# Decay rows of the first layer stored by head, with the mask and the first exponential held in written order

## The chip, the cores and the metric

The kernel runs on one core of one Trainium2 chip. The metric is device time in microseconds (us) of that core, from launch to end, as the median of the runs. Five engines work beside each other: TensorE (PE in the profile; PEld is its loading of weights), VectorE (DVE), ScalarE (ACT), GpSimd (POOL) and SyncE (SP), which issues most transfers. Each engine takes its own instructions strictly in order. An instruction that waits for another engine or for a transfer holds up everything behind it on its engine.

## The reference

A decoder of two layers over 1024 tokens with 1024 channels, in float32. The first layer is a gated delta rule with 8 heads; the second is windowed attention and has no part in this case. Cut to what matters here:

```python
q, k, v = split(silu(causal_conv(rms_norm(x) @ w_in)))     # per head: 128, 128 and 256 channels
beta = sigmoid(b);  g = -exp(A_log) * softplus(a + dt_bias) # log-decay by token and head
g = cumsum(g within a chunk)
decay = exp(where(tri, g[..., :, None] - g[..., None, :], -inf))
lower = where(strict, beta[..., :, None] * (k k^T) * decay, 0)
sol   = triangular_solve(I + lower, [v * beta, k * beta * exp(g)])
qk    = (q k^T) * decay
for each chunk:                                            # state S of a head
    v_new = u - w S
    o     = (q * exp(g)) S + qk v_new
    S     = S * exp(g_last) + (k * exp(g_last - g))^T v_new
x = x + (rms_norm(o) * silu(z)) @ w_out
```

So each head needs, for each of the kernel's 8 chunks of 128 tokens, a 128x128 table of exponentials of differences of summed decays. That table is what the change is about.

## The kernel before

TensorE does every product of the projections as three products of split operands (`whi`, `wlo` against `hh`, `hl`; lines 161 to 165). Its instructions run in the order in which the program writes them. On the other engines the framework's scheduler orders the work ahead of time, by priorities and by its own idea of when operands are ready, and it may put an instruction before one that was written earlier.

The first layer goes head by head. While the recurrence of head h (`head_delta`, line 613) runs, pieces of the projection of head h+1 (`head_in`, line 577) are put between its products (`interleave`, line 86), so that TensorE has something to do while the other engines prepare the next step. The recurrence has three stretches:

- the inverse of the chunk's triangle by doubling,
- the merge of two 64-blocks into one of 128 (lines 711 to 724), whose last step on ACT is the copy into `xt` at line 724,
- the scan over 8 chunks (lines 746 to 784). In each turn PE computes `sc` (line 759), ACT makes the rounded new values from it (`Z`, line 761), PE multiplies those into the state (lines 770 to 773), DVE adds them to the state `S` (line 776), ACT rounds it (`X`, line 781), and PE uses both in the next turn (lines 750 and 609 to 611).

The table of decays of a head, `dm`, is made in `decays` (line 568): SP loads the head's summed decays from DRAM (`gd`) to all 128 partitions, the same 4 KB for each (line 571), POOL masks the upper triangle (line 572), and ACT takes eight exponentials, one for each chunk (line 575). There are two buffers `dm`. The one for head h+2 is free when the merge of head h has split its own table (line 603, `dml<-dm`), and the scheduler puts load, mask and exponentials of head h+2 right there, in the scan of head h, long before they are used. So the first two loads run together at 95 us, and the other six come one in each scan of the first six heads.

ACT holds one table of functions at a time. A switch between the exponential and the silu of the convolution (lines 506, 529, 542) is an instruction of its own, ACT_TABLE_LOAD.

In `gd` the rows lie by chunk and head, row n*8+h, 512 bytes each. A head's load therefore reads, for each partition, eight pieces of 512 bytes, 4 KB apart.

Of the kernel before, what the change touches and what calls it, by code (L numbers as in the profile page):

```python
# [18 lines left out]
P = 128  # L19
T = 1024  # L20
# [6 lines left out]
# what the tensor engine is given to do, in us, while the other engines prepare a piece of the recurrence  # L27
# [29 lines left out]
def bucket_rows():  # L57
    """one-hot of the bucket of the distance (127 - u) mod 128, [32, 256]"""
    n = (127 - np.arange(256)) % P
    large = 16 + (np.log(np.maximum(n, 1) / 16) / np.log(128 / 16) * 16).astype(np.int64)  # L60
    bucket = np.where(n < 16, n, np.minimum(large, 31))
    return np.ascontiguousarray((np.arange(32)[:, None] == bucket[None, :]).astype(np.float32))


class Kernel:
# [5 lines left out]
    # work for the tensor engine is traced in the order it runs there: generators yield after every piece, and  # L71
    # pieces whose operands are still being made are put off by a number of ticks
# [13 lines left out]
    def interleave(self, front, back, share, ahead=100):  # L86
        """after each piece of front, as much of back as it asks for (times share); then what is left of back.
        What front puts on the other engines goes before what was traced shortly before it"""
        credit = 0.0
        while True:  # L90
            with self.tc.high_priority(offset=ahead):
                want = next(front, None)
            if want is None:
                break
            credit += want * share
            while credit > 1e-6:
                cost = next(back, None)
                if cost is None:
                    break
                credit -= cost  # L100
        for _ in back:
            pass
# [19 lines left out]
    def weight(self, src, shape, gain=None):  # L122
        """a block of weights, [128, shape] with 1024 numbers a row, as a sum of two float32r parts"""
        nc = self.nc
        assert shape[0] * shape[1] == 1024
        pool = self.wpools[self.wcount % len(self.wpools)]
        self.wcount += 1
        view = lambda t: t.rearrange("p (k c) -> p k c", k=shape[0])
        raw = view(self.wraw.tile([P, 1024], F32, name="wraw"))
        nc.sync.dma_start(raw, src)  # L130
        hi = view(pool.tile([P, 1024], F32R, name="whi"))
        lo = view(pool.tile([P, 1024], F32R, name="wlo"))
        if gain is None:
            nc.gpsimd.tensor_scalar(out=hi, in0=raw, scalar1=1.0, scalar2=1.0, op0=ALU.mult, op1=ALU.mult)  # L134
        else:
            nc.gpsimd.tensor_tensor(out=raw, in0=raw, in1=gain.unsqueeze(2).broadcast_to([P] + shape), op=ALU.mult)
            nc.scalar.copy(out=hi, in_=raw)
        (nc.gpsimd if self.wcount < 3 else nc.vector).tensor_tensor(out=lo, in0=raw, in1=self.f32(hi), op=ALU.subtract)  # L138
        return hi, lo

    def fetch(self):
        """the next block of weights, traced one block ahead of its use"""
        nxt = next(self.sources, None)
        if nxt is not None:
            self.ready.append(self.weight(*nxt))
# [9 lines left out]
    def gemm_ct(self, ps, w, half, ts=slice(0, 512)):  # L155
        """128 columns of the weights against half of the tokens, channels on the partitions"""
# [29 lines left out]
    def norm_half(self, half, xs, gain_col, tiles, stage, junk=None, wide=False, first=0):  # L186
        """[128,1024] token blocks, normalised in place; their split transposes go to self.hT[half], from block first
        on, by the eight steps that are returned. tiles: names of PSUM tiles to go round in; wide: on more than one
        engine"""
# [42 lines left out]
    # ---------------------------------------------------------------- first layer  # L232
# [123 lines left out]
    def gate_math(self, pt, dtb, nA):  # L356
# [6 lines left out]
        # softplus(a + dt_bias) = max(u,0) + 2 atanh(s), s = e/(2+e), e = exp(-|u|)  # L363
# [25 lines left out]
        # beta = 1/(1+exp(-b))  # L389
# [9 lines left out]
    def gate_sums(self):  # L399
# [9 lines left out]
        nc.scalar.copy(out=self.G.rearrange("p n h -> p (n h)"), in_=ps[:, 0, :])  # L409
        gl = ga.tile(sh, F32, name="gl")  # L410
# [14 lines left out]
    def gate_rows(self):  # L425
        """the summed decays by row, to DRAM, from where they come back broadcast"""
        nc = self.nc
        ps = self.dps.tile([P, 512], F32, name="tr")
        nc.tensor.transpose(out=ps[0:64, 0:P], in_=self.G.rearrange("p n h -> p (n h)"), identity=self.ident)
        rows = self.sm.tile([P, 512], F32, name="zs", bufs=4)  # L430
        nc.scalar.copy(out=rows[0:64, 0:P], in_=ps[0:64, 0:P])
        nc.sync.dma_start(self.gd, rows[0:64, 0:P])

    class ConvBlock:
        """one 128-column block of the projection, convolved; sink(half, acc) takes each half"""
# [43 lines left out]
    def head_blocks(self, h):  # L479
        """k, q blocks of a head; the tiles they fill are in self.nxt"""  # L480
# [20 lines left out]
        def q_sink(half, acc):  # L501
            hs = slice(half * 4, half * 4 + 4)

            def f():
# [5 lines left out]
                # the squares summed over the channels, by token: over 32 of them after a transposition of 32 x 32  # L510
                # blocks, then over the four groups of 32
# [55 lines left out]

    def decays(self, h, H):
        """exp of the summed decay between two tokens of a chunk"""
        nc, gd = self.nc, self.gd  # L570
        nc.sync.dma_start(H.dm, bass.AP(tensor=gd.tensor, offset=gd.offset + h * P, ap=[[0, P], [8 * P, NB], [1, P]]))
        nc.gpsimd.affine_select(out=H.dm, in_=H.dm, pattern=[[0, NB], [1, P]], compare_op=ALU.is_ge, fill=NEG,
                                base=0, channel_multiplier=-1)
        for n in range(NB):
            nc.scalar.activation(out=H.dm[:, n, :], in_=H.dm[:, n, :], func=AF.Exp, bias=self.mG[:, n, h:h + 1])

    def head_in(self, h, started=None):
        if started is None:
            k, q, v_sink = self.head_blocks(h)
            self.head_tiles(h)  # L580
            H = self.nxt
            for half in range(2):
                yield from k.half(half)
# [6 lines left out]
        for vb in range(2):  # L590
            v[vb] = self.ConvBlock(self, 16 + 2 * h + vb, v_sink(vb))
            for half in range(2):
                yield from v[vb].half(half)
                if (vb, half) == ((0, 0) if started is None else (1, 0)):
                    self.later(1, lambda: self.decays(h, H))
        self.cur = H

    def split(self, x, ph, hi, pl, lo):
        """x, a row of 128 by chunk, as two float32r parts"""
# [6 lines left out]
    def three(self, ps, wh, wl, mh, ml):  # L606
        """a float32 product of operands in two parts"""
# [5 lines left out]
    def head_delta(self, h, H):  # L613
# [3 lines left out]
        # -beta * kk * decay and qk * decay, both with the key's token on the partitions  # L617
# [13 lines left out]
        # the 64-blocks on the diagonal: inverse by doubling, from half-precision products  # L631
# [15 lines left out]
        def whole(d, x):  # L647
            """the same, both blocks in one product"""
# [41 lines left out]
        # two corrections in float32: E = I - (I + L) X, X' = X (I + E + E E)  # L690
# [19 lines left out]
        # 64 -> 128  # L710
# [17 lines left out]
        # scan over the chunks; the rows that come out take the place of the values  # L728
# [6 lines left out]
        def inside(n):  # L735
            """what the chunk's own tokens add to its rows"""
# [48 lines left out]
        # norm of the rows; the query's own norm enters through the guard  # L785
# [4 lines left out]
    def head_out(self, h, H, late):  # L790
        """normalised rows, transposed, with gain; gated unless the gate comes later"""
# [23 lines left out]
    def head_z(self, h, H, vbs=(0, 1)):  # L815
        """silu of the gate's columns, kept for head_out, or (no H) put on the rows that lie in DRAM"""
# [20 lines left out]
    # ---------------------------------------------------------------- projection back, with the residual  # L837
# [4 lines left out]
    def og_load(self, og, half, k4, tiles, raws):  # L842
        """four blocks of 128 rows, half of the tokens, in two float32r parts"""
# [10 lines left out]
    def out_proj(self, og, resid, cur, tiles, raws, px, acc, dst, finish):  # L854
        """og: [16, 128, T] rows by channel, the first half of the tokens loaded in cur; tiles(k4): room for the second;
        the sums go to dst, and finish(half, xs) takes them by four token blocks"""
# [34 lines left out]
    # ---------------------------------------------------------------- second layer  # L891
    def b_consts(self, st):
        """what the second layer needs of its small inputs, and the band of biases in DRAM"""
# [27 lines left out]
    def gemm_tc(self, ps, ws, n):  # L921
        """token block n against two weight blocks of 4 x 128 rows"""
# [36 lines left out]
    def key_stack(self, g):  # L959
        """keys of one head, transposed and split, twice over the partitions, in four steps"""  # L960
# [20 lines left out]
    class Group:  # L981
        """four query heads; they share their keys with the next or the last four"""
# [35 lines left out]
    def b_order():  # L1018
        """queries in time for their group; the gates half a group behind"""
# [17 lines left out]
    def b_q(self, X):  # L1037
        """the queries of four heads, normalised, by token"""
# [24 lines left out]
    def b_z(self, X, j):  # L1063
        """the gate's columns; silu of them goes on what attention gave when the whole group is there"""
# [18 lines left out]
    def b_attend(self, groups):  # L1083
        """attention; the blocks of 128 queries of four heads in a pipeline"""
# [23 lines left out]
        def logits(i):  # L1108
            """of the 128 keys that a query sees, those after it in its block's place stand for the block before"""
# [104 lines left out]
    def run(self):  # L1214
        nc, tc, I = self.nc, self.tc, self.I
        with ExitStack() as ctx:
# [4 lines left out]
            self.gd = dr.tile([NB * 8, P], F32, name="gd")  # L1221
# [75 lines left out]
    def weights(self):  # L1297
        """every block of weights in the order of its use"""
# [60 lines left out]
```

## Time and profile before

| | |
|---|---|
| time, median of 3 runs | 1937.23 us (1935.25 to 1937.33) |
| span of the profiled execution | 1937.3 us |
| time of that execution beside its span | not listed apart; its span is 0.07 us over the median of the runs |
| PE busy | 1840.0 us, 95% |
| DVE, ACT, POOL busy | 1228.7 us (63%), 816.4 us (42%), 528.7 us (27%) |
| six scans with a load of `dm` in them | the loads start at 151.82, 261.95, 370.83, 482.05, 592.53 and 701.33 us |
| loads of `dm` | 8 of 512 KB, 8.8 us from issue to landing (median) |

PE is busy nearly all the time, so what it loses is found in its waits, not in its share. An ACT or POOL that is idle costs nothing by itself; it costs when PE stands behind it.

### The profile page before, as it was taken

To read this page: it belongs to the slowest core of one execution; us is meant where nothing else is said; L and a number is where in the kernel's file an instruction comes from. 1 tells how busy PE (TensorE), PEld (TensorE's weight loads), DVE (VectorE), ACT (ScalarE), POOL (GpSimd) and SP (SyncE) were. 2 spreads that over 40 slices of the span, in tenths; PEclk is the share of its full clock that TensorE was granted. 3 is DMA by queue.
4 is the path that set the end of the run, shared out by engine and by line. 5 is a ranking of instruction groups with operands and counts; after the bars stand their busy time and mean duration, and the time that the engine had idled before them with its cause. 6 is when DMAs were issued, how large, how long until landed. Compare 5 with 4: busy or idle time off the path is not lost.

```text
span 1937.3 us, 33647 instructions
## 1 busy us (share of the span) xinstructions
PE 1840.0 (95%) x13186; PEld 1572.6 (81%) x13186; DVE 1228.7 (63%) x2859; ACT 816.4 (42%) x1947; POOL 528.7 (27%) x554
## 2 busy tenths in 40 slices
PE   5998999899899999989999999999999999999999
PEld 4676778687777878767899999888788887879999
DVE  6766776759576676875535256876776776753432
ACT  4545353434525353442202042457657667671100
POOL 2322232223122222221311232333333333322111
PEclk9999999999999999999999999999999999999999
DMA  4521111211121111111645331011111111216542
GB/s 145 122 54 33 55 34 55 45 33 47 31 66 33 55 34 39 61 43 62 218 163 179 109 99 55 23 50 44 61 40 50 50 34 60 69 58 201 180 172 85
DMA packets 157284, 147.62 MB, mean 76 GB/s; under 512 B 7115, under 2 KB 132549, under 8 KB 157125
## 3 DMA queue, kind: packets, MB, share of 16 engines
q1 hardware_dynamic: 146784, 128.30, 21.6%
q10 hardware_dynamic: 10340, 17.16, 2.8%
q8 instruction: 104, 1.70, 0.3%
q14 instruction: 56, 0.45, 0.1%
HBM read 115.00 MB, written 30.44 MB: 75 GB/s over the span
## 4 chain that ended last, share of the span: by engine, by line
PE 40%; DVE 5%; POOL 2%; issue 2%; ACT 2%; DMA 1%; POOLq 0%; ACTq 0%; SPq 0%; DVEq 0%
PE acc L876 6%; PE acc L878 6%; PE acc L877 6%; PE mm L928 4%; PE mm L930 3%; PE mm L929 3%; PE pv L1170 2%; PE mm L165 2%; PE mm L163 2%; PE mm L161 2%; PE tp L1149 1%; PE lg L1123 1%; PE lg L1124 1%; DMA wraw<-in_b_w_in 1%; DVE wlo L138 1%
## 5 line engine op out<-in xcount | busy, mean ns | idle before, releaser
L161 PE MATMUL mm<-hh,whi 128*128 128x512 f32 (+1 forms) x1040 | 428.1, 412 | 1.6 <-ACT hh L223 1.5
L163 PE MATMUL mm<-hl,whi 128*128 128x512 f32 (+1 forms) x1040 | 419.6, 403 | 1.0 <-DVE hl L224 0.7
L165 PE MATMUL mm<-hh,wlo 128*128 128x512 f32 (+1 forms) x1040 | 416.8, 401 | 0.0
L138 DVE TENSOR_TENSOR wlo<-wraw,whi 128x1024 fp32r<-128x1024 f32 x141 | 180.2, 1279 | 238.7 <-POOL whi L134 214.7
L134 POOL TENSOR_SCALAR whi<-wraw 128x1024 fp32r<-128x1024 f32 x112 | 121.2, 1082 | 466.1 <-PE acc L878 240.6
L165 PEld LDWEIGHTS mm<-hh,wlo 128*128 128x128 f32 x1040 | 198.2, 191 | 36.6 <-issue 4.2
L161 PEld LDWEIGHTS mm<-hh,whi 128*128 128x128 f32 x1040 | 198.0, 190 | 36.7 <-issue 4.8
L163 PEld LDWEIGHTS mm<-hl,whi 128*128 128x128 f32 x1040 | 198.6, 191 | 34.1 <-issue 4.2
L928 PE MATMUL mm<-whi,hh 128*128 128x256 f32 x608 | 180.4, 297 | 0.0
L461 DVE SCALAR_TENSOR_TENSOR acc<-u,cw,acc 128x512 f32<-128x512 f32 x192 | 162.7, 849 | 26.4 <-POOL acc L458 23.2
L930 PE MATMUL mm<-whi,hl 128*128 128x256 f32 x608 | 172.3, 283 | 0.0
L929 PE MATMUL mm<-wlo,hh 128*128 128x256 f32 x608 | 172.2, 283 | 0.0
L876 PE MATMUL acc<-whi,hh 128*128 128x256 f32 x512 | 145.0, 283 | 0.0
L877 PE MATMUL acc<-wlo,hh 128*128 128x256 f32 x512 | 144.9, 283 | 0.0
L878 PE MATMUL acc<-whi,hl 128*128 128x256 f32 x512 | 144.9, 283 | 0.0
L1139 ACT ACTIVATE lsb<-lsb,nm 128x128 f32<-128x128 f32 x256 | 99.9, 392 | 65.5 <-DVE se L1135 56.3
L928 PEld LDWEIGHTS mm<-whi,hh 128*128 128x128 f32 x608 | 116.1, 191 | 11.0 <-issue 10.8
L929 PEld LDWEIGHTS mm<-wlo,hh 128*128 128x128 f32 x608 | 116.3, 191 | 0.2
L930 PEld LDWEIGHTS mm<-whi,hl 128*128 128x128 f32 x608 | 116.0, 191 | 0.0
L458 POOL TENSOR_SCALAR acc<-u,cw 128x512 f32<-128x512 f32 x64 | 63.7, 995 | 185.5 <-ACT u L454 162.9
L1143 POOL TENSOR_TENSOR lsb<-lsb,den 128x512 f32<-128x512 f32 x64 | 68.4, 1069 | 152.6 <-ACT pT L1153 51.3
L876 PE MATMUL acc<-whi,oh 128*128 128x256 f32 x384 | 108.5, 283 | 0.0
(350 smaller groups left out, 4306.3 us busy)
## 6 DMA issues: line engine op xcount, KB each, us to landing
wraw<-in_a_w_in SPq DMA_DIRECT2D x48, 512.0 KB, 4.0
wraw<-in_a_w_out SPq DMA_DIRECT2D x32, 512.0 KB, 3.8
wraw<-in_b_w_in SPq DMA_DIRECT2D x32, 512.0 KB, 4.0
wraw<-in_b_w_out SPq DMA_DIRECT2D x32, 512.0 KB, 4.3
og<-zs SPq DMA_DIRECT2D x32, 256.0 KB, 2.0
ogT<-zs SPq DMA_DIRECT2D x28, 256.0 KB, 2.1
btab<-lt SPq DMA_DIRECT2D x1, 4096.0 KB
dm<-gd SPq DMA_DIRECT2D x8, 512.0 KB, 8.8
```

What stands on the lines that cost most here:

```text
L134: nc.gpsimd.tensor_scalar(out=hi, in0=raw, scalar1=1.0, scalar2=1.0, op0=ALU.mult, op1=ALU.mult)
L138: (nc.gpsimd if self.wcount < 3 else nc.vector).tensor_tensor(out=lo, in0=raw, in1=self.f32(hi), op=ALU.subtract)
L161: nc.tensor.matmul(ps, hi[:, k, :], hh[:, k, :], start=(k == 0), stop=False)
L163: nc.tensor.matmul(ps, hi[:, k, :], hl[:, k, :], start=False, stop=False)
L165: nc.tensor.matmul(ps, lo[:, k, :], hh[:, k, :], start=False, stop=(k == KT - 1))
L461: nc.vector.scalar_tensor_tensor(out=acc, in0=u[:, t:t + 512], scalar=cw[:, t, blk:blk + 1], in1=acc, op0=ALU.mult, op1=ALU.add)
L876: nc.tensor.matmul(po, oh[:, kk, ts], hi[:, kk, :], start=(k4 + kk + b == 0), stop=False)
L877: nc.tensor.matmul(po, oh[:, kk, ts], lo[:, kk, :], start=False, stop=False)
L878: nc.tensor.matmul(po, ol[:, kk, ts], hi[:, kk, :], start=False, stop=(k4 + kk + b == 7))
L928: nc.tensor.matmul(ps, hh[:, k, ts], hi[:, k % 4, :], start=(k == 0), stop=False)
L929: nc.tensor.matmul(ps, hh[:, k, ts], lo[:, k % 4, :], start=False, stop=False)
L930: nc.tensor.matmul(ps, hl[:, k, ts], hi[:, k % 4, :], start=False, stop=(k == KT - 1))
```

## The change

Three edits in the first layer.

1. The summed decays are copied once more, into `Gh`, with head before chunk, and that copy is transposed and stored. `gd` then lies by head, and a head's load reads one contiguous piece of 4 KB for each partition.
2. The load is written in a function of its own, `decays_load`, which `head_in` calls at the start of a head instead of after its first block of values (for the first head, started earlier, both still come together).
3. The mask and the first of the eight exponentials are marked `keep_in_program_order`: the scheduler keeps them behind the work of their engine that was written before them. The other seven exponentials remain free.

The rest of the diff takes out comments and shifts line numbers.

```diff
@@ gate_sums
         nc.scalar.copy(out=self.G.rearrange("p n h -> p (n h)"), in_=ps[:, 0, :])
+        self.Gh = ga.tile([P, 8, NB], F32, name="Gh")
+        nc.vector.tensor_copy(self.Gh.rearrange("p h n -> p n h"), self.G)
@@ gate_rows
-        nc.tensor.transpose(out=ps[0:64, 0:P], in_=self.G.rearrange("p n h -> p (n h)"), identity=self.ident)
+        nc.tensor.transpose(out=ps[0:64, 0:P], in_=self.Gh.rearrange("p h n -> p (h n)"), identity=self.ident)
...
-        nc.sync.dma_start(self.gd, rows[0:64, 0:P])
+        nc.sync.dma_start(self.gd.rearrange("h n c -> (h n) c"), rows[0:64, 0:P])
@@ decays
+    def decays_load(self, h, H):
+        gd = self.gd
+        self.nc.sync.dma_start(H.dm, bass.AP(tensor=gd.tensor, offset=gd.offset + h * T, ap=[[0, P], [1, T]]))
+
     def decays(self, h, H):
-        nc, gd = self.nc, self.gd
-        nc.sync.dma_start(H.dm, bass.AP(tensor=gd.tensor, offset=gd.offset + h * P, ap=[[0, P], [8 * P, NB], [1, P]]))
-        nc.gpsimd.affine_select(out=H.dm, in_=H.dm, pattern=[[0, NB], [1, P]], compare_op=ALU.is_ge, fill=NEG,
-                                base=0, channel_multiplier=-1)
+        nc, tc = self.nc, self.tc
+        cut = nc.gpsimd.affine_select(out=H.dm, in_=H.dm, pattern=[[0, NB], [1, P]], compare_op=ALU.is_ge, fill=NEG,
+                                      base=0, channel_multiplier=-1)
+        tc.keep_in_program_order(cut)
         for n in range(NB):
-            nc.scalar.activation(out=H.dm[:, n, :], in_=H.dm[:, n, :], func=AF.Exp, bias=self.mG[:, n, h:h + 1])
+            e = nc.scalar.activation(out=H.dm[:, n, :], in_=H.dm[:, n, :], func=AF.Exp, bias=self.mG[:, n, h:h + 1])
+            if n == 0:
+                tc.keep_in_program_order(e)
@@ head_in
             H = self.nxt
+            self.decays_load(h, H)
...
                 if (vb, half) == ((0, 0) if started is None else (1, 0)):
+                    if started is not None:
+                        self.later(1, lambda: self.decays_load(h, H))
                     self.later(1, lambda: self.decays(h, H))
@@ run
-            self.gd = dr.tile([NB * 8, P], F32, name="gd")
+            self.gd = dr.tile([AH, NB, P], F32, name="gd")
```

What the scheduler makes of it shows in the order of the instructions. First SP, from the store of the summed decays to the third scan's load; `wraw` are blocks of weights. Before:

```order
L432 DMA gd<-zs 64x128
L130 DMA wraw<-in_a_w_in 128x8x128 x2
L571 DMA dm<-gd 128x8x128 x2
L130 DMA wraw<-in_a_w_in 128x8x128 x3
L571 DMA dm<-gd 128x8x128
L130 DMA wraw<-in_a_w_in 128x8x128 x3
L810 DMA ogT<-zs 128x512 x4
```

The same stretch of SP in the changed kernel, where the load is line 572:

```order
L434 DMA gd<-zs 64x128
L130 DMA wraw<-in_a_w_in 128x8x128 x2
L572 DMA dm<-gd 128x1024 x2
L130 DMA wraw<-in_a_w_in 128x8x128 x3
L572 DMA dm<-gd 128x1024
L130 DMA wraw<-in_a_w_in 128x8x128 x3
L821 DMA ogT<-zs 128x512 x4
```

No load moves in SP's order, in this stretch or later; only the form of the load differs. POOL's order does not change either. PE's order differs in one name, the transposition of `Gh` in place of `G`.

Second ACT, in the second head, from the silu before the merge's last copy to the second turn of the scan. Here `xt` is the merged inverse, `Z` the rounded new values, `X` the rounded state, `junk` a sum of squares. Before:

```order
L542 ACTIVATE acc<-acc 128x512
L724 COPY xt<-kqp 64x8x64
L761 ACTIVATE Z<-sc,beta 128x256
L454 COPY u<-mm 128x512
L546 COPY vt<-tr 128x4x128
L781 CAST X<-S 128x256
L741 COPY vt<-kqp 128x256
L743 ACTIVATE junk_2720,sso<-vt 128x256
L575 ACT_TABLE_LOAD
L575 ACTIVATE dm<-dm,mG 128x128
L761 ACTIVATE Z<-sc,beta 128x256
```

The same stretch of ACT in the changed kernel, where the exponentials are line 581:

```order
L544 ACTIVATE acc<-acc 128x512
L581 ACT_TABLE_LOAD
L581 ACTIVATE dm<-dm,mG 128x128
L735 COPY xt<-kqp 64x8x64
L772 ACTIVATE Z<-sc,beta 128x256
L456 COPY u<-mm 128x512
L548 COPY vt<-tr 128x4x128
L792 CAST X<-S 128x256
L752 COPY vt<-kqp 128x256
L754 ACTIVATE junk_2722,sso<-vt 128x256
L581 ACTIVATE dm<-dm,mG 128x128 x3
L772 ACTIVATE Z<-sc,beta 128x256
```

The table load now stands in front of the merge's copy, with the eighth exponential of the table loaded one head earlier. At the old place stand three exponentials of the new table instead of one; the other four follow behind the second `Z` and one vector copy, and the silu with its table load behind them. In before the silu came at once and the table was switched a second time. The second to sixth head have this order. In the first head the new table's first exponential comes one turn later than before, and its old place is taken by the eighth exponential of the second head's table, which waits for nothing new. In the seventh head one exponential between two table loads is added in the scan. On DVE, beside the copy into `Gh`, the last step of a convolution goes behind the split of the new values in these scans.

## Rows read from the trace of the kernel before

**Rows 1.** PE's waits, 100 to 760 us: waiting tile <- releaser: us, times, longest

```profile
PE sc L770 <- ACT Z L761: 25.7, 5, 6.2
PE sc L750 <- DVE S L776: 7.3, 1, 7.3
```

**Rows 2.** timeline, second head's scan: start us, us, engine, line, operation, tiles, [idle <- releaser]

```profile
259.32 0.58 ACT L724 COPY xt<-kqp 64x512 f32<-64x512 f32 x1
...
259.96 0.70 PE L759 MATMUL sc<-vt,xt 128*128 128x256 f32 x2
...
261.95 0.37 SPq L571 DMA_DIRECT2D dm<-gd  x1
...
265.62 1.28 ACT L575 ACT_TABLE_LOAD   x1
...
270.75 1.09 POOL L572 TENSOR_SCALAR_AFFINE_SELECT dm<-dm 128x1024 f32<-128x1024 f32 x1 [6.88 <-DMA dm<-gd]
271.87 0.40 ACT L575 ACTIVATE dm<-dm,mG 128x128 f32<-128x128 f32 x1 [4.97 <-POOL dm L572]
272.18 0.45 ACT L761 ACTIVATE Z<-sc,beta 128x256 fp32r<-128x256 f32 x1
...
272.69 0.58 PE L770 MATMUL sc<-Z,w 128*128 128x256 f32 x1 [4.77 <-ACT Z L761]
...
273.02 1.28 ACT L542 ACT_TABLE_LOAD   x1
...
274.31 0.63 ACT L542 ACTIVATE acc<-acc 128x512 f32<-128x512 f32 x1
```

**Rows 3.** timeline, first head's scan

```profile
151.82 0.37 SPq L571 DMA_DIRECT2D dm<-gd  x1
...
160.64 1.09 POOL L572 TENSOR_SCALAR_AFFINE_SELECT dm<-dm 128x1024 f32<-128x1024 f32 x1 [10.52 <-DMA dm<-gd]
...
166.22 0.47 DVE L776 SCALAR_TENSOR_TENSOR S<-S,egl,sc 128x256 f32<-128x256 f32 x1
...
166.75 1.22 PE L750 MATMUL sc<-S,kq 128*128 128x256 f32 x2 [7.31 <-DVE S L776]
```

**Rows 4.** 8 us windows: us, busy by engine (x), PEclk, DMA share, GB/s

```profile
166.75:174.75 8.00, 8.00 (x36) 6.72 (x37) 3.36 (x8) 5.22 (x14) 0.26 (x1) 0.80 0.00 0
272.69:280.69 8.00, 8.00 (x37) 6.87 (x38) 2.70 (x7) 6.79 (x14) 0.20 (x1) 0.81 0.00 1
382.50:390.50 8.00, 8.00 (x30) 6.77 (x31) 2.66 (x6) 5.46 (x11) 0.00 (x0) 0.63 0.00 0
494.21:502.21 8.00, 8.00 (x36) 6.87 (x37) 2.61 (x6) 6.61 (x13) 0.03 (x1) 0.79 0.01 2
602.96:610.96 8.00, 8.00 (x36) 6.77 (x37) 2.67 (x6) 6.55 (x13) 0.00 (x0) 0.79 0.00 0
711.84:719.84 8.00, 8.00 (x34) 6.86 (x35) 2.67 (x6) 6.25 (x12) 0.00 (x0) 0.73 0.01 3
804.81:812.81 8.00, 6.52 (x33) 5.12 (x34) 6.52 (x14) 3.97 (x10) 0.86 (x3) 1.00 0.42 133
896.81:904.81 8.00, 8.00 (x34) 6.61 (x34) 3.03 (x7) 2.83 (x9) 0.00 (x0) 0.79 0.28 98
```

**Rows 5.** timeline of PE, two short stops later in the layer

```profile
804.81 0.35 PE L770 MATMUL sc<-Z,w 128*128 128x256 f32 x1 [1.40 <-ACT Z L761]
...
896.81 1.07 PE L750 MATMUL sc<-S,kq 128*128 128x256 f32 x2 [1.13 <-DVE S L779]
```

**Rows 6.** DMA issues of the page: tiles, engine, count, KB each, us to landing

```profile
wraw<-in_a_w_in SPq DMA_DIRECT2D x48, 512.0 KB, 4.0
...
dm<-gd SPq DMA_DIRECT2D x8, 512.0 KB, 8.8
```

**Rows 7.** GB/s in 40 slices while one decay load runs alone, 152.9 to 159.9 us

```profile
GB/s 91 91 88 88 94 82 38 91 88 88 91 67 23 88 85 94 61 91 88 53 0 35 91 91 82 82 76 94 56 85 94 94 76 64 82 111 9 0 61 82
```

**Rows 8.** GB/s in 40 slices of one weight load, 247.6 to 250.1 us

```profile
GB/s 0 0 82 82 139 147 156 131 172 156 82 131 131 156 139 188 238 279 352 344 344 352 344 344 360 328 360 352 336 352 344 344 328 246 238 131 74 66 41 0
```

## Prediction

> **What bounds the kernel now.** I read three views: first PE's waits over the first layer, then the timeline of the scans in which those waits lie, then the granted clock behind them. PE is the engine to watch because every other one has slack over the layer. Its waits from 100 to 760 us show two large entries: five stops of 25.7 us in all for `Z`, and one of 7.3 us for `S` [rows 1]. That is 33.0 us in six stops, one for each load of `dm` that falls in a scan.
>
> The timeline of the second head's scan shows the chain of the five. SP issues the load at 261.95. POOL's mask starts at 270.75, 8.80 later, when the load has landed. ACT has already switched its table (265.62) and stands before the first exponential until 271.87. `Z` is behind it on ACT and starts at 272.18, and PE restarts at 272.69 after 4.77 us of nothing [rows 2]. PE was therefore ready at 267.92, 5.97 after the issue. With S for the time from issue to mask, the stop is S + 1.12 + 0.82 - 5.97 = S - 4.03; S of 8.80 gives 4.77, as shown.
>
> In the first head's scan the chain goes another way: the mask waits on POOL, a convolution step queues behind it on POOL, its three steps on DVE come next, and `S` is behind those. Issue 151.82, mask 160.64, `S` 166.22, PE at 166.75 after 7.31 [rows 3]. With S = 8.82 that stop is S - 1.51.
>
> After each stop PE runs for some microseconds at a granted clock below full: the six windows of 8 us read 0.80, 0.81, 0.63, 0.79, 0.79 and 0.73 [rows 4], between the levels of 1.2 and 2.4 GHz. The missing shares add to 1.45, times 8 us is 11.6 us. So the loads cost 33.0 + 11.6 = 44.6 us of the span now.
>
> **The change part by part.**
>
> *The load is not issued earlier.* SP's order is the same, and the load still waits for the split of the older table on DVE, since the buffer is free only then. Neither the new function nor the pin of the mask moves anything on SP or POOL. What is left of the transfer is its length.
>
> *One piece of 4 KB instead of eight of 512 bytes.* A load of weights of the same 512 KB, also in 512-byte pieces, lands in 4.0 us, a load of `dm` in 8.8 [rows 6]. Alone on the queues the `dm` load flows mostly at an even 82 to 94 GB/s [rows 7], while the weights reach 344 to 360 [rows 8]. Size and pieces are equal, so the difference lies in the source: 128 partitions read the same eight pieces, 4 KB apart. The changed load reads the same 4 KB as one run. No row shows such a load. The bounds are 4.0 us if the run spreads over the memory as the weights do, and 8.8 if reading the same 4 KB by all is what is slow. I take S = 4.0: the even rate, a quarter of the other, looks like pieces that meet at a few places because of their pitch, and the new layout has no pitch. Both ends are kept for the range.
>
> The Trainium skill speaks against this part ("DMA: Bandwidth & Descriptors", Specifications): pieces from 512 B up already run at line rate. The weights' 344 to 360 GB/s agree [rows 8], so longer pieces as such would win nothing; by that rule alone S stays at 8.8, and it is the first rival below.
>
> *The table load in front of the merge's copy* (second to sixth head). Before, the copy into `xt` starts at 259.32 and PE's next product at 259.96, with nothing to spare [rows 2]. Now a table load (1.28) and one exponential stand before it. An exponential costs 0.31 from its start to the next instruction (271.87 to 272.18), so the copy and all of the scan behind it come 1.6 us later. PE stops that long in five heads: 5 x 1.6 = 8.0 us. The cover is gone here: PE's filler is written in a fixed order and used up. The bound below is 0, if PE had the slack after all.
>
> On table loads the skill names more ("ScalarE: Activation LUTs", What ACT_TABLE_LOAD costs): 1283 ns and then about 1380 ns of drain. Here the silu starts 1.29 after its table load began (273.02 to 274.31) [rows 2], so no drain shows; with it the five copies would cost some 7 us more, an estimate from that page.
>
> *Three exponentials instead of one before* `Z`: two more, 0.62. PE needs `Z` 1.6 later as well, so the new stop is (S + 1.12 + 0.82 + 0.62) - (5.97 + 1.6) = S - 5.0, and nothing below S = 5.0. ACT itself is ready for the exponential about 5.3 after the issue (265.62 plus 1.6, without the old table load), which gives `Z` 0.8 before PE needs it.
>
> *The rounded state* `X` *comes later*, behind four exponentials (1.25), a table load (1.28) and the silu (0.6), where the silu alone with its table load stood. I count some 4.0 us from `Z` to `X`; PE reaches the products with `X` about as late. Nothing is charged; if it misses, it costs up to 0.5 per head.
>
> *The first head* keeps its chain through POOL and DVE: S - 1.5 = 2.5 us at S = 4.0.
>
> *The clock in the new kernel.* One stop of 1.13 us is followed by a window at 0.79, another of 1.40 by one at 1.00 [rows 4, 5]. So a short stop may cost nothing or (1 - 0.79) x 8 = 1.7. I charge 1.7 once for the first head's 2.5 and a third of it for each of the five: 1.7 + 2.8 = 4.5.
>
> *Small things.* The copy into `Gh` stands once before PE's transposition; it is a quarter as wide as the 0.47 us update of `S` [rows 3], so at most 0.3. The table loads and exponential added in the seventh head meet ACT where it has about 1 us to spare: 0.4. The moved convolution steps on DVE cost nothing; they let the new values pass first.
>
> Sum at S = 4.0: 2.5 + 8.0 + 4.5 + 0.7 = 15.7 where 44.6 stood, so 28.9 less. The span is 1937.3 and the median 1937.23, the same for this purpose: **1908 us**.
>
> **The rivals.**
>
> *The load stays as long* (S as now). For it: all partitions still read one 4 KB, and the skill's rule above. Against it: the even, low rate that weights in like pieces don't have. Then each of the five heads has S - 5.0 + 1.6 = S - 3.4 in place of S - 4.03, 0.63 more, 3.1 in all, with 0.7 of small things: 1941, slower than before. The mechanism is the switch of the table that now holds the merge's copy, unpaid. It decides as long as the load is shortened by less than 3.8/6 = 0.6 us, that is, lands after 8.2.
>
> *The load is half repaired*, S of 6 to 7. For it: a contiguous run may still be read by all queues at the same spots at once. At 6.5 the first head stops 5.0, the five 1.6 + 1.5 each, 15.5, and all six stops bring the slow clock, 10.2: 31.4 with the small things, 13 less, 1924.
>
> *The load gets longer*, since 16 queues now walk through the same run in step. For it: nothing but the form. At S = 12 the first head stops 3.2 longer, the five 3.5 longer (8.6 against 25.7/5 = 5.1): with small things 21.4 more, 1959.
>
> *The merge's wait is covered*, S = 4.0 but the copy costs PE nothing: 8.0 and 2.8 less, 1898. Against it: the 0.64 between copy and product.
>
> **How the numbers follow.** The forecast (S from 3.8 to 5, slow clock after none or all of the stops, 1903 to 1915) has 0.62, the covered merge 0.02, the half repair 0.18 (S of 7.5 gives 1930), the unchanged load 0.14, the longer one 0.04. Two per mille, 3.9 us, is about what a measurement tells from no change. Faster are the first three, 0.82; the unchanged load at +3.8 lies on that line, 0.08 of it within and 0.06 beyond; so same 0.08, slower 0.10. The range takes in the forecast and the half repair and leaves out the rest, 0.20: 1902 to 1932.
>
> **What would show it.** Landing of `dm<-gd` near 4 us and 250 GB/s or more during it: the step on the layout. PE's wait for `Z` in five scans near zero, and in its place a wait of some 1.6 us for `xt` before the product of line 759: the steps on ACT. The wait for `S` in the first head near 2.5. Slow-clock windows fewer than six in the scans. If the load lands at 8 or later, the forecast is wrong in its first step; if it lands at 4 and the time is still above 1920, the merge or `X` was mispriced.

## The result and the profile after

The changed kernel takes 1908.03 us (median of 4 runs, 1906.83 to 1909.14); the kernel before takes 1936.32 beside it (1935.25 to 1937.33). The ratio is 0.9851, with a 95% interval of 0.9837 to 0.9865. The gain is 28.3 us. The profiled execution took 1906.83 us with a span of 1905.1.

The row of `dm` among the page's DMA issues of the changed kernel, with the weights beside it (columns as in [rows 6]):

```profile
wraw<-in_a_w_in SPq DMA_DIRECT2D x48, 512.0 KB, 3.9
...
dm<-gd SPq DMA_DIRECT2D x8, 512.0 KB, 3.7
```

A load of `dm` now lands as early as a load of weights of the same size, 3.7 us after its issue where it was 8.8.

PE's waits of the changed kernel from 100 to 760 us, which answer to [rows 1]:

```profile
PE sc L770 <- ACT xt L735: 8.5, 5, 1.7
PE sc L770 <- DVE r L763: 4.1, 5, 0.8
PE sc L784 <- DVE lh L773: 3.1, 6, 1.4
PE sc L761 <- DVE S L787: 2.5, 1, 2.5
...
```

Entries of 1.5 us and less are left out. The wait for `Z`, 25.7 us before, is gone from the list. The first head's wait for `S` has shrunk from 7.3 to 2.5. Two of these entries are new, both five times: `xt`, 8.5 us in all, and `r` (the values less what the state already holds of them), 4.1. Waits for `lh` were there before too, with the same 3.1. So 33.0 us of stops in the six scans have become 15.1 (8.5, 4.1 and 2.5).

The timeline of the second head's scan in the changed kernel, which answers to [rows 2], shows where both new waits come from:

```profile
255.17 1.28 ACT L581 ACT_TABLE_LOAD   x1
256.47 0.40 ACT L581 ACTIVATE dm<-dm,mG 128x128 f32<-128x128 f32 x1
256.89 0.58 ACT L735 COPY xt<-kqp 64x512 f32<-64x512 f32 x1
257.53 0.70 PE L770 MATMUL sc<-vt,xt 128*128 128x256 f32 x2 [1.70 <-ACT xt L735]
...
257.82 0.34 SPq L572 DMA_DIRECT2D dm<-gd  x1
...
261.03 1.48 DVE L138 TENSOR_TENSOR wlo<-wraw,whi 128x1024 fp32r<-128x1024 f32 x1
...
261.65 1.81 POOL L577 TENSOR_SCALAR_AFFINE_SELECT dm<-dm 128x1024 f32<-128x1024 f32 x1 [0.21 <-DMA dm<-gd]
...
262.43 1.30 DVE L793 TENSOR_TENSOR XT<-S,X 128x256 fp32r<-128x256 f32 x1
...
263.49 0.98 ACT L581 ACTIVATE dm<-dm,mG 128x128 f32<-128x128 f32 x3 [0.33 <-POOL dm L577]
263.66 0.47 DVE L763 SCALAR_TENSOR_TENSOR r<-sc,neG,vt 128x256 f32<-128x256 f32 x1
...
264.18 0.70 PE L770 MATMUL sc<-r,xt 128*128 128x256 f32 x2 [0.82 <-DVE r L763]
...
264.92 0.47 ACT L772 ACTIVATE Z<-sc,beta 128x256 fp32r<-128x256 f32 x1 [0.44 <-PE sc L770]
```

The table load and one exponential stand in front of the copy into `xt`: 255.17 to 256.89 is 1.72 us, and PE stops 1.70 for it. The mask starts 3.83 after the load's issue, and `Z` starts when PE has made `sc`, not when the exponentials let it. Between them lies the second new wait: `XT` on DVE takes 1.30 us beside the mask, `r` is behind it, and PE stops 0.82.

The first head's scan in the changed kernel, which answers to [rows 3]:

```profile
153.91 0.34 SPq L572 DMA_DIRECT2D dm<-gd  x1
...
157.82 1.09 POOL L577 TENSOR_SCALAR_AFFINE_SELECT dm<-dm 128x1024 f32<-128x1024 f32 x1 [5.61 <-DMA dm<-gd]
...
163.49 0.47 DVE L787 SCALAR_TENSOR_TENSOR S<-S,egl,sc 128x256 f32<-128x256 f32 x1
...
164.02 0.70 PE L761 MATMUL sc<-S,kq 128*128 128x256 f32 x2 [2.50 <-DVE S L787]
```

The chain is the old one with a load 4.9 us shorter (3.91 from issue to mask), and the stop is 2.50.

The granted clock behind the stops, in windows of 8 us of the changed kernel (columns as in [rows 4]):

```profile
164.02:172.02 8.00, 8.00 (x45) 6.90 (x46) 4.68 (x12) 6.70 (x19) 1.05 (x1) 1.00 0.00 0
...
264.18:272.18 8.00, 8.00 (x44) 6.96 (x45) 4.62 (x9) 6.86 (x17) 0.58 (x1) 1.00 0.19 58
```

Both read 1.00 where [rows 4] read 0.80 and 0.81. Of the 44.6 us that the loads cost before, 15.1 are left: 29.5 less. Medians give 28.3, the two profiled spans 32.2. The profile before is of a long execution: every run takes 1.7 to 2.0 us more than its span, so a span of 1937.3 goes with a time of some 1939 (an estimate), 2.7 above the median.

### The profile page after: what moved, and what is told of

Same layout as the page of the kernel before. It is cut to its first block, busy times and chain, and to the rows that moved or that the text cites. A ratio compares the mean times of both kernels' runs of the same rounds, so it can differ in the third digit from the quotient of the medians.

```text
span 1905.1 us, 33635 instructions
## 1 busy us (share of the span) xinstructions
PE 1828.6 (96%) x13186; PEld 1562.9 (82%) x13186; DVE 1229.2 (65%) x2860; ACT 807.5 (42%) x1939; POOL 536.5 (28%) x554
## 4 chain that ended last, share of the span: by engine, by line
PE 36%; DVE 8%; ACT 3%; POOL 3%; issue 2%; DMA 1%; POOLq 0%; SPq 0%; ACTq 0%; DVEq 0%
PE acc L887 6%; PE acc L889 6%; PE acc L888 6%; PE mm L939 3%; PE mm L940 3%; PE mm L941 3%; PE pv L1181 2%; ACT lsb L1150 1%; PE mm L165 1%; PE mm L163 1%; PE mm L161 1%; DVE lsb L1140 1%; DVE wlo L138 1%; POOL lsb L1154 1%; PE tp L1160 1%
## 5 line engine op out<-in xcount | busy, mean ns | idle before, releaser
L161 PEld LDWEIGHTS mm<-hh,whi 128*128 128x128 f32 x1040 | 197.0, 189 | 36.9 <-issue 5.2
```

The lines of the kernel that those rows point to most:

```text
L161: nc.tensor.matmul(ps, hi[:, k, :], hh[:, k, :], start=(k == 0), stop=False)
```

## The experiments

**The layout alone, the order alone, and both, on one chip.** The first kernel is the one before with only the layout; ACT keeps the order of before.

```diff
+        self.Gh = ga.tile([P, 8, NB], F32, name="Gh")
+        nc.vector.tensor_copy(self.Gh.rearrange("p h n -> p n h"), self.G)
...
-        nc.sync.dma_start(H.dm, bass.AP(tensor=gd.tensor, offset=gd.offset + h * P, ap=[[0, P], [8 * P, NB], [1, P]]))
+        nc.sync.dma_start(H.dm, bass.AP(tensor=gd.tensor, offset=gd.offset + h * T, ap=[[0, P], [1, T]]))
...
```

> The kernel before with the summed decays stored by head and nothing else of the change; ACT has the order of before (no table load in front of the merge's copy). Theory A (the length of the load earns everything, the order on ACT costs): dm lands about 3.7 us after issue as in the changed kernel; no wait for xt and none for r; the wait for Z in five scans is S + 1.1 to 1.9 (mask) + 0.8 - 6.0, that is 0 to 0.6 each; the first head stops 2.5; at most one slow-clock window (1.7). 1937 - 44.6 + 2.5 + 0 to 3 + 0 to 1.7 + 0.3 = 1895 to 1900, 8 to 13 below the changed kernel. Rival B (the new order on ACT, which takes the table load out of the scan's turn, earns a part of it): 1908 or more, with waits for Z of 1 us or more left.

The second is the changed kernel with the old layout:

```diff
-        self.Gh = ga.tile([P, 8, NB], F32, name="Gh")
...
-        self.nc.sync.dma_start(H.dm, bass.AP(tensor=gd.tensor, offset=gd.offset + h * T, ap=[[0, P], [1, T]]))
+        self.nc.sync.dma_start(H.dm, bass.AP(tensor=gd.tensor, offset=gd.offset + h * P, ap=[[0, P], [8 * P, NB], [1, P]]))
...
```

> The changed kernel with the old layout of the summed decays: ACT and DVE have the order of the changed kernel, the load still reads eight pieces of 512 bytes, 4 KB apart. Theory A: dm lands after 8.8 as before; the wait for xt of 1.7 in five heads, and Z stops S - 5.0 = 3.8 or somewhat less behind it; together 5.5 against 5.1 per head: 1939 (1936 to 1945), no gain. Rival B: the order alone earns a part, 1920 to 1930.

The third is the changed kernel once more, beside them.

> The changed kernel once more, on the same chip as the two halves of the change: 1907 to 1909. Theory A: the two halves add up, (layout alone - before) + (order alone - before) = (both - before) within 8 us, where the order's part is smaller with the long load since the stop for Z then absorbs most of the later merge.

| kernel | median us | ratio to before (95%) | issue to mask, median of six scans |
|---|---|---|---|
| before | 1938.41 | | 8.8 |
| layout alone | 1901.56 | 0.981 (0.9797 to 0.9824) | 3.6 |
| order alone | 1940.83 | 1.0015 (1.0004 to 1.0026) | 8.8 |
| both (the change) | 1909.58 | 0.9849 (0.9836 to 0.9862) | 3.8 |

PE's waits from 95 to 765 us with the layout alone (`Z` is line 763 here, `S` 778, `lh` 764):

```profile
PE sc L775 <- DVE lh L764: 5.4, 11, 1.4
PE sc L752 <- DVE S L778: 2.5, 1, 2.5
...
PE sc L772 <- ACT Z L763: 0.4, 2, 0.2
```

The same with the order alone:

```profile
PE sc L779 <- ACT Z L770: 20.2, 5, 5.1
PE sc L768 <- ACT xt L733: 8.5, 5, 1.7
PE sc L759 <- DVE S L785: 7.3, 1, 7.3
...
```

The layout earns 36.9 us; the new order earns nothing and costs. With the short load it costs 8.0 us (1909.58 - 1901.56); with the long one 2.4, because the stop for `Z` takes up most of what the later merge loses: 20.2 + 8.5 + 7.3 = 36.0 of stops against 33.0. Theory A holds, rival B falls. Three figures miss A's by a little: the layout alone lies 1.6 us above A's 1895 to 1900, though 8.0 below the changed kernel as expected (8 to 13); the changed kernel lies 0.6 above its 1907 to 1909; and with the order alone `Z` stops 4.0 in the mean, where 3.8 or less was expected. The two effects add to -34.4, both together measure -28.8; the gap of 5.6 is the difference between those two prices of the order. In its own way the moved order gives a little: with the layout alone the convolution on DVE stands before the split of the new values, and the waits for `lh` are 5.4 instead of 3.1.

The wait for `r` stands in neither of the two lists, the lines left out included; only both halves together bring it. In stops the order costs with the short load 8.5 for `xt` and 4.1 for `r`, less the 2.3 of `lh` and 0.4 of `Z` that the layout alone has more: 9.9, where the medians say 8.0. The second scan with the layout alone, for comparison with the timeline above (line 784 is `XT`, 754 is `r`, 574 the mask):

```profile
257.80 0.34 SPq L573 DMA_DIRECT2D dm<-gd  x1
...
259.29 1.48 DVE L138 TENSOR_TENSOR wlo<-wraw,whi 128x1024 fp32r<-128x1024 f32 x1
...
260.69 0.41 DVE L784 TENSOR_TENSOR XT<-S,X 128x256 fp32r<-128x256 f32 x1
...
261.03 0.47 DVE L754 SCALAR_TENSOR_TENSOR r<-sc,neG,vt 128x256 f32<-128x256 f32 x1
...
261.27 1.09 POOL L574 TENSOR_SCALAR_AFFINE_SELECT dm<-dm 128x1024 f32<-128x1024 f32 x1 [1.57 <-DMA dm<-gd]
```

The scan runs 1.7 us earlier against the load, so the mask starts after `XT` and takes 1.09.

**The mask in two halves.** This asks whether the mask is what makes `XT` and `r` late. On the changed kernel:

```diff
-        cut = nc.gpsimd.affine_select(out=H.dm, in_=H.dm, pattern=[[0, NB], [1, P]], ...
-        tc.keep_in_program_order(cut)
+        for j in range(2):
+            part = H.dm[:, j * 4:j * 4 + 4, :]
+            cut = nc.gpsimd.affine_select(out=part, in_=part, pattern=[[0, 4], [1, P]], ...
+            tc.keep_in_program_order(cut)
```

> The changed kernel with the mask on POOL cut into two instructions of four chunks each, at the same place in POOL's order; DVE's order is unchanged, on ACT one exponential stands one place earlier. Theory M (the new wait for r, 0.8 us in five heads, comes from the rounding remainder XT on DVE, which takes 1.30 instead of 0.41 us while the mask runs on POOL, one instruction holding up the other for its whole length): XT ends after at most one half of the mask, 0.7 to 0.9, the wait for r falls to 0.3 to 0.5 in each head, and the time by 1.5 to 2.5 us. Rival N (DVE is simply full there, behind the split of the weights of 1.48 us): XT and the wait for r stay at 1.30 and 0.8, time unchanged within 1.

Its second scan (line 579 is the mask, 795 `XT`, 765 `r`):

```profile
259.99 1.48 DVE L138 TENSOR_TENSOR wlo<-wraw,whi 128x1024 fp32r<-128x1024 f32 x1
...
260.51 2.23 POOL L579 TENSOR_SCALAR_AFFINE_SELECT dm<-dm 128x512 f32<-128x512 f32 x2
...
261.40 0.85 DVE L795 TENSOR_TENSOR XT<-S,X 128x256 fp32r<-128x256 f32 x1
...
262.17 0.47 DVE L765 SCALAR_TENSOR_TENSOR r<-sc,neG,vt 128x256 f32<-128x256 f32 x1
...
262.69 0.70 PE L772 MATMUL sc<-r,xt 128*128 128x256 f32 x2 [0.37 <-DVE r L765]
```

`XT` takes 0.85 instead of 1.30, PE stops 0.37 instead of 0.82, and over the five heads the wait for `r` is 1.8 us instead of 4.1. Theory M holds for the wait: DVE's subtraction behind the mask waits for the instruction on POOL, and a shorter instruction holds it for less. The time does not prove it: 1907.56 us, 0.9836 (0.982 to 0.9851), is 2.0 below the changed kernel in the table, as expected, but its interval overlaps that of the whole mask.

**What was slow in the old load.** Six kernels are the one before with nothing but the distance of the rows in `gd` changed, in the one store and in the loads. Each load still reads eight pieces of 512 bytes per partition, and no instruction moves. The edit for 4608 bytes (1152 numbers); the others differ in this number:

```diff
-        nc.sync.dma_start(self.gd, rows[0:64, 0:P])
+        nc.sync.dma_start(self.gd[:, 0:8 * P].rearrange("n (h c) -> n h c", c=P), rows[0:64, 0:P])
...
-        nc.sync.dma_start(H.dm, bass.AP(tensor=gd.tensor, offset=gd.offset + h * P, ap=[[0, P], [8 * P, NB], [1, P]]))
+        nc.sync.dma_start(H.dm, bass.AP(tensor=gd.tensor, offset=gd.offset + h * P, ap=[[0, P], [1152, NB], [1, P]]))
...
-            self.gd = dr.tile([NB * 8, P], F32, name="gd")
+            self.gd = dr.tile([NB, 1152], F32, name="gd")
```

> The kernel before with the rows by chunk set 4608 bytes apart instead of 4096; a head's load still reads eight pieces of 512 bytes for each partition, and the instructions are those of before. Theory P (the eight pieces of a head meet at one place, since they are a multiple of 4 KB apart): dm lands in about 4 us and the kernel runs like the layout alone, 1895 to 1900. Rival Q (pieces of 512 bytes, read by all partitions, are slow as such): dm lands in 8.8 and the time is 1936.

> The kernel before with the rows by chunk set 6144 bytes apart; pieces of 512 bytes, instructions of before. With 4608 the load ran at 333 to 358 GB/s, with 4096 at 82 to 94. Theory P (pieces meet where their places agree modulo 4 KB): at 6144 the eight pieces lie at two places modulo 4 KB, so about twice the rate of before, 160 to 190 GB/s, mask 5 to 6 us after issue; the stops for Z are 1 to 2 us in five heads, and the time 1903 to 1915. Rival R (only the number of different places modulo 1 KB or less decides, or any pitch but 4096 is good): the mask starts after 3.8 us and the time is 1896 to 1902.

> The kernel before with the rows by chunk set 8192 bytes apart. Theory P: one place modulo 4 KB, so no better than before: mask 8.4 to 8.9 us after issue, 80 to 95 GB/s, 1934 to 1941 us. If places are told apart by 8 KB or more, or 4096 alone is bad, it is worse or better than that: 12 us or 4 us.

> The kernel before with the rows by chunk 4608 bytes apart, timed in rounds: it keeps ACT's order of before and needs no copy by head. One execution gave 1898.87. Theory A: as fast as the layout by head alone (1901.6) within 3 us, 1897 to 1902, so below the changed kernel by 7 to 11. If contiguity of 4 KB had a worth of its own, it would be slower than the layout alone by more than 3.

> The kernel before with the rows by chunk 4224 bytes apart, 128 more than before; pieces of 512 bytes. The loads so far: 333 to 358 GB/s at a pitch of 4608, 141 to 218 at 6144, 82 to 94 at 4096, about 42 at 8192. Theory D (the rate halves with each doubling of the largest power of two that divides the pitch, up to the full rate): 4224 is a multiple of 128 only, so full rate, mask 3.8 us after issue, 1895 to 1903. Rival G (what counts is how far the places of the eight pieces spread modulo 4 KB, in grains of 512 bytes or more): they spread over 1.4 KB in place of 4, so two to three grains, 170 to 260 GB/s, mask 4.5 to 6 us after issue, 1900 to 1915.

> The kernel before with the rows by chunk 16384 bytes apart. Theory D: the rate halves once more, some 21 GB/s, so 25 us for 512 KB and the mask 27 us after issue; each of six scans stops 12 us longer than at 8192 and the first two loads come later too: 2055 to 2085. Rival E (at 8192 all pieces meet at one place already): the rate stays at 42, the time at 1985 to 1992.

> The kernel before with the rows by chunk 8320 bytes apart, 128 more than 8192. The runs at 4096, 4224, 4608, 6144, 8192 and 16384 fit one picture (theory H): addresses 8 KB apart meet, in places of 512 bytes, and the place on which most of a head's 4 KB falls sets the time, 42 to 44 GB/s for all of it on one place. At 8320 the eight pieces begin 0, 128, ... 896 into the 8 KB; the fullest place gets 2048 of the 4096 bytes, as at 4096, so 82 to 94 GB/s, mask 8.4 to 9 us after issue, 1933 to 1941 us, like the kernel before at twice its pitch. Rival D (only the power of two in the pitch counts, here 128): mask after 3.8 us, 1895 to 1903.

| pitch, bytes | issue to mask, median of six scans | time, us |
|---|---|---|
| 4096 (before) | 8.8 | 1938.41 |
| 4608 | 3.9 | 1898.87, once; 1897.75 timed, 0.9795 (0.9775 to 0.9815) |
| 4224 | 5.6 | 1913.23, once |
| 6144 | 5.7 | 1916.65, once |
| 8192 | 14.7 | 1987.81, once |
| 8320 | 11.0 | 1959.76, once |
| 16384 | 14.4 | 1986.11, once |

The kernel before took 1938.41 to 1941.02 us beside these runs. The rate shows the difference most plainly. GB/s in 40 slices, with the count of packets under it, at a pitch of 4608, 256.1 to 260.1 us; the load is the first two thirds of the row:

```profile
GB/s 0 0 51 123 77 72 143 236 292 317 338 333 358 353 348 333 348 333 307 287 236 143 82 82 21 20 10 0 0 0 0 0 41 133 154 128 77 56 154 256
DMA packets 1235, 0.62 MB, mean 156 GB/s; under 512 B 16, under 2 KB 1235, under 8 KB 1235
```

At 6144, 259.6 to 264.4 us (a weight load follows at the end of the row):

```profile
GB/s 0 0 43 38 154 183 218 205 183 183 166 183 171 141 162 171 192 149 196 175 175 68 26 154 175 158 124 183 230 175 154 107 85 77 119 201 235 213 260 354
```

At 8192, 284.1 to 298.1 us (again with weights at the end):

```profile
GB/s 0 34 45 41 48 9 35 66 32 42 25 56 42 48 44 44 38 54 42 41 41 23 48 41 47 39 53 42 41 42 44 42 19 61 60 143 135 217 300 274
```

With [rows 7], the distances 4608, 6144, 4096 and 8192 give four levels, each about half of the one above: some 345, 175, 88 and 42 GB/s. The two distances that are 128 bytes off lie between: some 150 GB/s at 4224 (260.6 to 265.4 us) and 60 at 8320 (273.7 to 283.9 us). At 4608 no packet has 2 KB or more, and all but 16 are pieces of 512 bytes; they flow at the rate of the weights in [rows 8]. So rival Q falls: neither the length of the pieces nor 128 partitions that read the same bytes is slow by itself. What counts is where the eight pieces lie against each other.

How the places are told apart went through three theories. "Modulo 4 KB" fell at 8192, which should have been like 4096. "Each doubling of the power of two in the pitch" fell at 16384, which is no slower than 8192, and at 4224, a multiple of 128 only, which is not at full rate. "Modulo 8 KB, in places of 512 bytes, by the fullest place" was made from six of the pitches and fits them; tried on a new one, 8320, it expected 8.4 to 9 us and got 11.0, while the power of two would have given 3.8. The coarse picture, that pieces which lie close to each other modulo 8 KB slow each other, agrees with all seven distances, but it was read from them and no run shows the mechanism. The size of a place remains open, and so does where `gd` begins in memory. Nor does a run show whether a load in which every partition reads rows of its own would suffer at these distances.

The times follow the loads; 4608 is inside the range expected of it, 4224 and 16384 inside that of a rival (G and E), 6144 is 1.7 us above its own, and 8192 and 8320 are far outside theirs. The pitch of 4608 needs neither `Gh` nor the new order and runs at 1897.75 us (1894.59 to 1904.05). It beats both kernels of the change; next to the layout alone (0.981, overlapping intervals) no difference can be claimed.

## Why the prediction was right, point by point

*The load is not issued earlier, and becomes as short as a load of weights.* Right: SP's place for the load is the same, and S was taken as 4.0 and is 3.7 in the median of the six scans (3.56 to 3.91). The reason given was the pitch, and the runs with other pitches show that it sets the rate; that the pieces meet at a few places is how these runs are read, not shown. The rule weighed against it, that pieces from 512 bytes up run at line rate, agrees with the 333 to 358 GB/s at 4608; it does not speak of where the pieces lie.

Another place of the Trainium skill does ("DMA: Bandwidth & Descriptors", Latency and other measured facts): large powers of two as a distance of rows cost rate, and some padding restores it. It gives that for copies of 16 KiB a row at distances from 512 KiB up; here 4 and 8 KB already show it, with 88 and 42 GB/s, and 512 bytes of padding on 4 KB restore 345.

*The stop for* `Z` *goes.* Right: S - 5.0 is below nothing, and no wait for `Z` is left in these scans.

*The merge's copy stops PE 1.6 us in five heads, 8.0.* Right in place and size: 1.70 each, 8.5. The order alone has the same 8.5 with the old layout, the layout alone has none of it. Which of the two pins moves the table load no run shows; POOL, where the mask runs, kept its order.

*The first head, 2.5.* Right: 2.50, and 2.5 with the layout alone.

*The rounded state* `X` *comes 4.0 after* `Z`*, and nothing is charged.* Right: 264.92 to 268.78 in the changed kernel, 3.9, and PE has no wait for it.

*The clock, 4.5.* Wrong in size: the profiled execution has no slow window in the six scans. In the second profile of the same kernel one follows the first head's stop, at 0.50:

```profile
162.30:165.70 3.40, 3.34 (x9) 2.80 (x10) 1.25 (x4) 1.08 (x4) 0.00 (x0) 0.50 0.00 0
```

That is 1.7 us, as charged for the first head. The stop before it, in that profile's list of PE's waits, was shorter than the 2.5 of the first:

```profile
PE sc L761 <- DVE S L787: 2.1, 1, 2.1
```

The 2.8 charged for the five short stops were nothing: stops of 1.7 us left the clock at 1.00 in both.

*Small things, 0.7.* Too high by 0.4: PE's transposition waits 0.8 us for the copy into `Gh`, where it waited 0.5 for `G` before, so the copy costs the 0.3 estimated for it; in the seventh head no new wait of PE shows.

*What no step had.* The wait for `r`, 4.1 us. The prediction priced the mask at 1.12 from rows in which it ran alone, and moved the scan 1.6 us later and the mask 5 earlier without asking what DVE does when they meet. They met at `XT`. By itself this error would have made the forecast 4 us too low; the clock, charged 4.5 and costing none in this execution, made it up. So the sum, 15.7 predicted and 15.4 found (15.1 of stops and 0.3 for `Gh`), is closer than its parts: of its terms the load, the merge, and the first head are right by themselves, and that two errors of 4 us with opposite signs cancel is luck. The prediction also took the span of 1937.3 and the median of 1937.23 for the same; by the estimate above, its waits are those of an execution some 2 us longer than that median.

The range and the side were carried by the load. Of the rivals, the one with the unchanged load has its price borne out by the order alone: +3.8 us was worked out, +2.4 measured (by its interval, 0.8 to 5.0).

## What to carry to other kernels

When a load flows at an even low rate while one of the same size and pieces flows at four times that, suspect its addresses: change the distance of its rows by one piece before you reorder anything. Half of a change can cost what the other half hides, and a timing of both together does not show it; run the halves alone. When one chain is shifted against another, look for what now lies beside each other, on the engines that share something, and not only for what waits in a queue.

## What the runs showed of the hardware that was not expected

- In these scans the mask on POOL and a two-operand subtraction on DVE hold each other up by whole instructions. In the changed kernel's second head the mask starts at 261.65, during DVE's two-operand subtraction, which ends at 262.51; it ends at 263.46, 0.95 later. `XT`, another such subtraction, starts at 262.43 and ends at 263.73, 0.27 after the mask. Alone the two take 1.09 and 0.41. In five scans the mask took 1.81 to 2.07. Halving the mask moved the ends as whole instructions would (`XT` 0.85). The Trainium skill ("SBUF — State Buffer", Who interferes with whom) says that a VectorE instruction with two inputs in SBUF and a GpSimd instruction that reads SBUF take a shared port as an exclusive lock; the trace agrees.
- The rate of a broadcast load fell to 42 GB/s from one distance of rows alone (8192 bytes), and the kernel to 1987.81 us, slower than before by 49, without a moved instruction.
- Stops of PE of 1.7 us left the granted clock at full in both profiles of the changed kernel, although a stop of 1.13 was followed by a window at 0.79 in the kernel before [rows 4, 5]. The first head's stop was followed by the lower level in one of the two, and that was the shorter one (2.1 us against 2.5). So in these traces the length of a stop alone does not tell whether the clock falls.
